# Issuing the table loads of the state space model's pairs from GpSimd in place of SyncE

## The chip, the core and the metric

The program runs on one core of one Trainium2 chip. The metric is the device time of one execution, in microseconds (us), over the median of several executions. The core has the engines TensorE (PE in the profile, with its weight loads as PEld), VectorE (DVE), ScalarE (ACT), GpSimd (POOL) and SyncE (SP). Each of them takes its instructions strictly in the order in which they were put into its queue; an instruction that waits holds up all that stands behind it on the same engine. In this kernel SyncE computes nothing: it issues DMA transfers.

## The reference

Two layers of a hybrid backbone over 640 tokens (128 context, 512 latent). In each layer one input projection feeds three head groups that run beside each other: a state space model (SSM), neighbourhood attention and grouped query attention. One output projection and a gated feed-forward network follow. The SSM is a diagonal complex recurrence in 16 groups of 16 channels with 64 states, run forward and backward:

```
def ssm_mixer(u, lp, h0_f, h0_b):
    ...
    for d, (h0, rev) in ...:
        lam_bar, b_bar = ssm_discretize(lp['ssm_lam_re'][d], lp['ssm_lam_im'][d], ...)
        hs = ssm_scan(uf, lam_bar, b_bar, h0, rev)
        y = y + jnp.einsum('blgp,gcp->blgc', hs, c_mat).real
        finals.append(hs[:, 0] if rev else hs[:, -1])
    g = jax.nn.gelu(y.reshape(b, n, SSM_WIDTH))
    out = g * jax.nn.sigmoid(g @ lp['w_ssm_glu'])
```

## The kernel before

The kernel is one program for both layers. Weights come from HBM through SyncE (`wload`, L293 to L302, and others), are split by ScalarE and by VectorE or GpSimd into a rounded high part and a low remainder (`split`, L280 to L284: the high part on L283, the remainder on L284), and are multiplied on TensorE in three passes (`mm3`, L309 to L313). On GpSimd, L284 is the remainder for a part of the weights; in groups called `wl` it feeds the third pass.

The SSM (`ssm`, L669) works in chunks: 640 tokens are 80 columns of 8 tokens, and the 16 groups are taken as 8 pairs. `ssm_tables` (L429) computes the tables of each pair ahead and stores them in DRAM: V (input to state, 128x512), R (rotation, 128x320), C (state to output, 128x512) and Z (the part within a chunk, two times 128x8x16). For each pair:

- `front` (L692 to L718) takes three buffers a, b, c of one pool of ten (`k4`). It loads V and C into b (L697, L699) and R and Z into a (L698, L709 twice). Z is read in pieces of 64 bytes, 128x8 of them in each of its two loads. GpSimd copies the decay factors into a third part of a (L703) and clears four columns of them (L705, two instructions). PE multiplies the inputs with V (L714); ScalarE copies the result into c (L716).
- `turn` transposes it on PE (L724). `rotate` works on DVE: L732 and L738 rotate, the scan on L742 is the recurrence (it reads the copied and cleared factors of a), L747, L748 and L753 rotate back.
- `back` multiplies on PE with C (L767, 8 matmuls, which the profile counts as 16) and Z (L770, 2, counted as 4); ScalarE copies the result out (L772).

`front` of the next pair is put after `turn` of the current one. Ten buffers are few: b of a pair comes free when L767 of the pair two before is done, and a when L770 of it is done (for pair 6, a was held by a bias table that DVE's L948 reads).

The order of the instructions on every engine is set by the Tile framework: the program is written in stages that yield to each other (`layer`, L1358, runs the grouped query attention with the SSM's pairs, weight pieces of the input projection and the modulation weights between its steps, and then the neighbourhood attention with the last pairs), and a scheduler with a timeline of its own sets the final order from it (`schedule_with_timeline_sim=True`, L1911). So a change of one engine moves instructions on the others too.

Beside the SSM the profile's rows name: L381, modulation weights `wa` on PE; L859, transposes; L942 to L953, L978 and L853, neighbourhood attention; L1266, a store of ScalarE's tile `zt`.

Of the kernel before, what the change touches and what calls it, by code (L numbers as in the profile page):

```python
# [157 lines left out]
class Build:  # L158
# [510 lines left out]
    def ssm(self, l, zu, T, out):  # L669

        nc, I = self.nc, self.I
        V, S, G = nc.vector, nc.scalar, nc.gpsimd
# [3 lines left out]
        for m in range(2):  # L676
            ug = self.k4()[:, 0:SLAB].rearrange("p (g j) -> p g j", g=8)
            src = zu[m * 128:(m + 1) * 128].rearrange("(g c) (t j) -> t c g j", c=16, t=8)
# [13 lines left out]
        def front(pair):  # L692
            a, b, c = self.k4(), self.k4(), self.k4()
            rot, rml, tm = a[:, 0:320], a[:, 320:640], a[:, 640:896]
            tv, tcb = b[:, 0:512], b[:, 512:1024]
            vs = c[0:NJ, 0:512]
            nc.sync.dma_start(tv, T["V"][pair])  # L697
            nc.sync.dma_start(rot, T["R"][pair].rearrange("p w d e -> p (w d e)"))  # L698
            nc.sync.dma_start(tcb, T["C"][pair])  # L699
            r8 = T["r8"][:, 2 * pair:2 * pair + 2].unsqueeze(2).unsqueeze(3).broadcast_to([128, 2, 2, NJ])  # L700

            rv = rml.rearrange("p (d w j) -> p d w j", d=2, w=2)
            G.tensor_copy(rv, r8)  # L703
            for d, e in ((0, 16), (1, 64)):
                G.memset(rv[:, d, :, 0:e + 1:e], 0.0)  # L705
            for gg in range(2):
                zz = T["Z"][2 * pair + gg]
                src = bass.AP(tensor=zz.tensor, offset=zz.offset, ap=[[16, 128], [256, 8], [1, 16]])
                nc.sync.dma_start(tm[:, gg * 128:(gg + 1) * 128].rearrange("p (t c) -> p t c", t=8), src)  # L709
            g0 = (pair % 4) * 2  # L710
            ug = ugs[pair // 4][:, g0:g0 + 2, :]
            sp = self.psM()
            for gg in range(2):
                nc.tensor.matmul(sp[0:NJ, gg * 256:(gg + 1) * 256], lhsT=ug[:, gg, :],  # L714
                                 rhs=tv[:, gg * 256:(gg + 1) * 256], start=True, stop=True)
            S.copy(vs.rearrange("p (q g n) -> p g q n", q=4, g=2), sp[0:NJ].rearrange("p (g q n) -> p g q n", g=2, q=4))  # L716
            return rot.rearrange("p (w d e) -> p w d e", w=2, d=2), rml, tcb, tm, ug, vs, c
# [42 lines left out]
        def back(pair, sx, rot, rml, tcb, tm, ug, vs, c):  # L760
# [10 lines left out]
            for hf in range(2):  # L771
                S.copy(ysb[hf][0:NJ, :, pair * 32:(pair + 1) * 32].rearrange("p t (g c) -> p g t c", g=2),  # L772
                       yp.rearrange("p g (t c) -> p g t c", t=8)[:, :, hf * 4:hf * 4 + 4, :])

        nxt = front(0)
        yield
        sx = None
        for pair in range(NPAIR):
            cur = nxt
            vt = turn(*cur)  # L780
            if pair + 1 < NPAIR:
                nxt = front(pair + 1)
            sx = rotate(pair, vt, *cur)
            yield
            back(pair, sx, *cur)
            if pair + 1 < NPAIR:
                yield
# [16 lines left out]
        for hf in range(2):  # L804
            for ch in range(2):
# [4 lines left out]
                src = pt[:, 0:4 * NJ].rearrange("p (t j) -> p t j", t=4)  # L810
# [1104 lines left out]
```

## Time and profile before

| | us |
|---|---|
| median of 3 executions | 1797.16 (1796.97 to 1809.3) |
| profiled execution, its own time | 1788.01 |
| its span | 1786.0 |
| PE busy | 1641.2 (92%) |
| DVE busy | 1222.5 (68%) |
| ACT busy | 827.3 (46%) |
| POOL busy | 763.5 (43%) |
| mean granted clock of TensorE | 0.96 |

The profiled execution is 9 us below the median of the others. Matmuls overlap by their pipeline, so a busy share of 92% on PE does not say that 8% could be had. The SSM's pairs run in two stretches: their loads are issued from 163.8 to 320.8 us in layer 0, and in layer 1 from 1042.3 us (pair 0 alone), and then from 1088.2 to 1202.4 us. The rest of the time holds projections and the feed-forward network.

### The profile page before, as it was taken

The numbers are of one execution on the slowest core, as the hardware profiler recorded it, in microseconds if no ns is written. First come the engines' busy times: TensorE is split into PE (matmuls) and PEld (weight loads), VectorE is DVE, ScalarE is ACT, GpSimd is POOL, SyncE is SP. The second block draws the span as 40 slices with busy tenths as digits, with TensorE's granted clock in tenths as the row PEclk, the third lists the DMA queues.
The fourth block names the chain that finished last, engine by engine and source line by source line (L and its number), as shares of the span: only waits on it lengthen the run. The fifth ranks groups of instructions, "written<-read, shape, count | busy, mean of one in ns | idle before, by whom it ended". The sixth has DMA issues, their size and how long they took to land. (4 is left out here: it accounts for less than half of the span.)

```text
span 1786.0 us, 31489 instructions
## 1 busy us (share of the span) xinstructions
PE 1641.2 (92%) x11624; PEld 1435.8 (80%) x11624; DVE 1222.5 (68%) x2460; ACT 827.3 (46%) x1800; POOL 763.5 (43%) x651
## 2 busy tenths in 40 slices
PE   5899899898899999999897989998979999999997
PEld 2898677676788888798796978876859899998995
DVE  5765546627678776778877565565487687876777
ACT  5444446657443334243345556665574242433433
POOL 3853203059235343346266232111785254454463
PEclk9999899798999999999999999998989999999999
DMA  9445767446353645232324243463542231222212
GB/s 335 112 126 139 238 194 213 123 158 203 107 172 122 195 127 182 81 121 71 121 85 157 92 129 96 111 187 115 180 148 85 94 107 59 92 74 69 98 62 81
DMA packets 183114, 234.90 MB, mean 132 GB/s; under 512 B 78960, under 2 KB 112048, under 8 KB 182960
## 3 DMA queue, kind: packets, MB, share of 16 engines
q1 hardware_dynamic: 182960, 232.88, 42.3%
q8 instruction: 92, 1.51, 0.3%
q14 instruction: 62, 0.51, 0.1%
HBM read 203.57 MB, written 29.39 MB: 130 GB/s over the span
## 5 line engine op out<-in xcount | busy, mean ns | idle before, releaser
L284 POOL TENSOR_TENSOR wl<-wr,wh 128x512 fp32r<-128x512 f32 x362 | 504.2, 1413 | 522.8 <-ACT wh L283 343.2
L283 ACT CAST wh<-wr 128x512 fp32r<-128x512 f32 x450 | 275.2, 619 | 383.9 <-DVE wr L1597 88.6
L311 PE MATMUL psM<-hh,wh 128*128 128x320 f32 x560 | 180.3, 322 | 2.3 <-DVE ys L1647 1.1
L313 PE MATMUL psM<-hh,wl 128*128 128x320 f32 x560 | 177.9, 318 | 0.0
L312 PE MATMUL psM<-hl,wh 128*128 128x320 f32 x560 | 177.8, 318 | 0.0
L311 PEld LDWEIGHTS psM<-hh,wh 128*128 128x128 f32 x560 | 108.5, 194 | 6.2 <-issue 1.8
L311 PE MATMUL psT<-hh,wh 128*128 128x320 f32 x352 | 109.9, 312 | 0.0
L313 PEld LDWEIGHTS psM<-hh,wl 128*128 128x128 f32 x560 | 108.6, 194 | 1.5 <-issue 1.4
L312 PE MATMUL psT<-hl,wh 128*128 128x320 f32 x352 | 109.2, 310 | 0.0
L313 PE MATMUL psT<-hh,wl 128*128 128x320 f32 x352 | 109.0, 310 | 0.0
L312 PEld LDWEIGHTS psM<-hl,wh 128*128 128x128 f32 x560 | 108.7, 194 | 0.3
L230 POOL TENSOR_TENSOR sm<-sm,mhalf 128x1 f32<-128x1 f32 (+2 forms) x46 | 54.3, 1182 | 92.3 <-DVE sm L260 49.3
L1647 DVE TENSOR_TENSOR ys<-ys,psM 128x320 f32<-128x320 f32 x140 | 65.0, 481 | 33.8 <-PE psM L313 31.9
L1160 DVE TENSOR_REDUCE psS<-psS 128x1 f32<-128x640 f32 x64 | 52.7, 828 | 47.4 <-PE psS L1157 45.6
L1647 DVE TENSOR_TENSOR ys<-ys,psT 128x320 f32<-128x320 f32 x140 | 65.0, 481 | 28.8 <-PE psT L313 27.7
L311 PE MATMUL psT<-b,wh 128*128 128x320 f32 x240 | 76.5, 319 | 8.3 <-DVE ys L1647 7.4
L311 PE MATMUL psM<-b,wh 128*128 128x320 f32 x240 | 76.1, 317 | 5.8 <-DVE ys L1647 5.8
L284 POOL TENSOR_TENSOR wl<-ws,wh 128x512 fp32r<-128x512 f32 x40 | 53.6, 1340 | 64.4 <-ACT wh L283 62.6
L859 PE MATMUL psT<-ident,ys 128*128 128x128 f32 x440 | 73.2, 285 | 5.8 <-DVE hl L284 3.3
L311 PE MATMUL psM<-wh,xs 128*128 128x512 f32 x190 | 74.9, 394 | 3.7 <-DVE k L1771 3.5
L311 PE MATMUL psT<-wh,xs 128*128 128x512 f32 x190 | 75.6, 398 | 2.9 <-DVE k L1771 2.9
L1597 DVE TENSOR_TENSOR ws<-wr,wr 128x512 f32<-128x512 f32 x40 | 37.0, 926 | 58.9 <-DMA wr<-in_w_ffn_in_dram 28.3
(440 smaller groups left out, 4907.9 us busy)
## 6 DMA issues: line engine op xcount, KB each, us to landing
wr<-in_w_ffn_in_dram SPq DMA_DIRECT2D x88, 512.0 KB, 3.7
ev<-in_w_ada_dram SPq DMA_DIRECT2D x112, 256.0 KB, 4.0
wr<-in_w_ffn_out_dram SPq DMA_DIRECT2D x40, 512.0 KB, 3.9
wr<-in_w_out_dram SPq DMA_DIRECT2D x32, 512.0 KB, 3.6
wr<-in_w_in_dram SPq DMA_DIRECT2D x28, 512.0 KB, 4.8
wa<-in_w_ada_dram SPq DMA_DIRECT2D x24, 512.0 KB, 4.7
k<-in_x_dram SPq DMA_DIRECT2D x10, 512.0 KB, 5.6
xs<-zqk SPq DMA_DIRECT2D x32, 160.0 KB, 3.7
```

The source lines that it names most:

```text
L230: self.nc.gpsimd.tensor_tensor(out=o, in0=v, in1=self.mhalf.broadcast_to([128, v.shape[1]]), op=ALU.pow)
L283: nc.scalar.copy(hi, src)
L284: (lo_eng or nc.vector).tensor_tensor(out=lo, in0=src, in1=hi.bitcast(F32), op=ALU.subtract)
L311: nc.tensor.matmul(ps, lhsT=ah, rhs=bh, start=first, stop=False)
L312: nc.tensor.matmul(ps, lhsT=ah, rhs=bl, start=False, stop=False)
L313: nc.tensor.matmul(ps, lhsT=al, rhs=bh, start=False, stop=last)
L859: self.nc.tensor.transpose(pt[:, j * 128:(j + 1) * 128], s, self.ident)
L1160: V.tensor_reduce(out=m, in_=sp[:, :, 0:320], axis=AX.XY, op=ALU.max, negate=True)
L1597: V.tensor_tensor(out=o, in0=x, in1=y, op=op)
L1647: V.tensor_tensor(out=o, in0=x, in1=y, op=ALU.add)
```

## The change

The five loads of `front` are issued by GpSimd (`G` is `nc.gpsimd`) in place of SyncE. Eight pairs in two layers make 80 transfers.

```
-            nc.sync.dma_start(tv, T["V"][pair])
-            nc.sync.dma_start(rot, T["R"][pair].rearrange("p w d e -> p (w d e)"))
-            nc.sync.dma_start(tcb, T["C"][pair])
+            G.dma_start(tv, T["V"][pair])
+            G.dma_start(rot, T["R"][pair].rearrange("p w d e -> p (w d e)"))
+            G.dma_start(tcb, T["C"][pair])
...
-                nc.sync.dma_start(tm[:, gg * 128:(gg + 1) * 128].rearrange("p (t c) -> p t c", t=8), src)
+                G.dma_start(tm[:, gg * 128:(gg + 1) * 128].rearrange("p (t c) -> p t c", t=8), src)
```

Three places show how the order moved. The first is GpSimd's queue at the last two pairs of layer 0. `k_697` and `k_696` are the buffers b and a of pair 6, `k_711` and `k_710` those of pair 7; `xs_4044` belongs to the attention.

```order
+L697 DMA k_697_3842<-tabV_306 128x512
+L699 DMA k_697_3842<-tabC_307 128x512
 L891 MEMSET xs_4044 128x64
+L698 DMA k_696_3841<-tabR_309 128x320
 L703 COPY k_696_3841<-r_65_310 128x320
+L709 DMA k_696_3841<-tabZ_308 128x8x16 x2
+L697 DMA k_711_3936<-tabV_306 128x512
+L699 DMA k_711_3936<-tabC_307 128x512
+L698 DMA k_710_3935<-tabR_309 128x320
+L703 COPY k_710_3935<-r_65_310 128x320
+L709 DMA k_710_3935<-tabZ_308 128x8x16 x2
 L705 MEMSET k_696_3841 128x2x2 x2
```

Before, the two memsets of pair 6 (last row) followed the copy of pair 6 at once; now Z of pair 6 and all that pair 7 loads stand between them. Layer 1 has the same order at its last two pairs.

The second place is PE's queue between the first matmul of pair 7 and L767 of pair 6 in layer 0. `k_711` and `k_697` are again b of pairs 7 and 6, `k_698` the buffer c with the result of pair 6's scan; the other rows are the attention's.

```order
+L859 MATMUL psT_4071<-ident,ys_3873 128x128 x4
+L714 MATMUL psM_3946<-k_711_3936,k_433_2377 80x256 x2
+L859 MATMUL psT_4077<-ident,ys_3873 128x128 x2
+L859 MATMUL psT_4158<-ident,ys_3967 128x128 x4
+L724 MATMUL psM_4107<-ident,k_712_3937 128x80 x4
+L978 MATMUL psT_4077<-ys_4070,xs_3757 64x128 x4
+L978 MATMUL psT_4077<-ys_4070,k_672_3751 64x128 x2
+L853 MATMUL psT_4077<-ident,sm_3889 64x128 x2
 L767 MATMUL psS_4094<-k_697_3842,k_698_3843 80x128
```

L714 and L724 of pair 7 stood ahead of L767 of pair 6 before too, some rows earlier; the rows of L859, L978 and L853 stood behind it. In layer 1 six such rows of L859 moved ahead of L767 of pair 6.

The third place is GpSimd's queue at pair 4 of layer 0, with `k_621` and `k_620` as its b and a. The rows of L284 are remainders of weights.

```order
 L284 TENSOR_TENSOR wl_3234<-wr_3231,wh_3233 128x512
+L697 DMA k_621_3438<-tabV_306 128x512
+L698 DMA k_620_3437<-tabR_309 128x320
+L699 DMA k_621_3438<-tabC_307 128x512
+L703 COPY k_620_3437<-r_65_310 128x320
+L709 DMA k_620_3437<-tabZ_308 128x8x16 x2
 L284 TENSOR_TENSOR wl_3238<-wr_3231,wh_3237 128x512
 L284 TENSOR_TENSOR wl_4451<-wr_4448,wh_4450 128x512
-L703 COPY k_620_3437<-r_65_310 128x320
```

The pair's loads now stand ahead of the remainder `wl_3238`, which before followed `wl_3234` directly. On PE its first use stands 64 rows behind the last row of L767 of pair 2; before, it stood 13 rows behind.

## Rows read from the trace of the kernel before

**Rows 1.** The page: span, and busy time of each engine.

```profile
span 1786.0 us, 31489 instructions
PE 1641.2 (92%) x11624; PEld 1435.8 (80%) x11624; DVE 1222.5 (68%) x2460; ACT 827.3 (46%) x1800; POOL 763.5 (43%) x651
```

**Rows 2.** Windows: start:end, length, busy PE, PEld, DVE, ACT, POOL, clock, DMA.

```profile
163.00:345.00 182.00, 162.13 (x1544) 131.41 (x1542) 107.31 (x267) 94.07 (x247) 34.15 (x52) 0.93 0.71 203
1088.00:1204.00 116.00, 112.29 (x962) 97.55 (x961) 72.66 (x188) 72.18 (x191) 22.90 (x39) 0.97 0.53 144
```

**Rows 3.** Waits of PE, 163 to 345 us: total, times, longest.

```profile
PE psM L381 <- DMA wa<-in_w_ada_dram: 6.4, 5, 2.5
```

**Rows 4.** Waits of SP's queue, the same stretch.

```profile
SPq L697 <- PE psS L767: 7.4, 3, 4.4
```

**Rows 5.** Lines L697 and L709: issue, ns minimum/median/maximum, first to last start.

```profile
L697 SPq DMA_DIRECT2D k<-tabV x16: 319/370/1170, 163.8 to 1199.8; - x16
L709 SPq DMA_DIRECT2D k<-tabZ x32: 425/532/1034, 171.0 to 1202.4; - x32
```

**Rows 6.** DMA issues: KB each, median us from issue to landing.

```profile
k<-tabV SPq DMA_DIRECT2D x16, 256.0 KB, 3.3
k<-tabZ SPq DMA_DIRECT2D x32, 64.0 KB, 4.0
```

**Rows 7.** Groups of POOL by shape: busy us, mean ns, idle before.

```profile
L284 POOL TENSOR_TENSOR wl<-wr,wh 128x512 fp32r<-128x512 f32 x362 | 504.2, 1413 | 522.8 <-ACT wh L283 343.2 <-DVE wl L284 113.7 <-DMA ev<-in_w_ada_dram 33.0
...
L703 POOL COPY k<-r 128x320 f32<-128x320 f32 x16 | 8.7, 545 | 59.1 <-PE psS L770 30.1 <-DMA tabC<-k 15.5 <-DVE ys L948 8.8
...
L705 POOL MEMSET k<- 128x4 f32 x32 | 2.3, 105 | 0.8
```

**Rows 8.** Timeline of layer 0's last pairs: start, length, engine; SP and POOL.

```profile
316.63 0.32 SPq L698 DMA_DIRECT2D k<-tabR  x1
316.67 0.45 POOL L703 COPY k<-r 128x320 f32<-128x320 f32 x1 [1.02 <-DVE ys L948]
```

**Rows 9.** The same stretch: DVE, from the scan of pair 6.

```profile
326.56 0.82 DVE L742 TENSOR_TENSOR_SCAN k<-k,xs 128x320 f32<-128x320 f32 x1
...
327.54 0.48 DVE L747 TENSOR_TENSOR xs<-k,k 128x320 f32<-128x320 f32 x1
...
329.20 0.69 DVE L753 TENSOR_TENSOR k<-xs 128x80 f32<-128x80 f32 x4
```

**Rows 10.** The same stretch: PE, from L767 of pair 6.

```profile
331.01 0.71 PE L767 MATMUL psS<-k,k 64*80 64x128 f32 x2
...
338.81 0.66 PE L859 MATMUL psT<-ident,ys 128*128 128x128 f32 x4
...
340.36 0.66 PE L978 MATMUL psT<-ys,xs 128*64 128x128 f32 x8
...
341.39 0.50 PE L942 MATMUL psS<-b,b 128*128 128x256 f32 x2
```

**Rows 11.** Layer 1: copy of pair 6 on POOL, L767 of pair 6 on PE.

```profile
1196.34 0.45 POOL L703 COPY k<-r 128x320 f32<-128x320 f32 x1 [7.76 <-DVE ys L948]
...
1212.70 0.71 PE L767 MATMUL psS<-k,k 64*80 64x128 f32 x2
```

**Rows 12.** Pair 4 of layer 0: L767 of pair 2, and PE's spacing.

```profile
274.17 0.44 PE L767 MATMUL psS<-k,k 64*80 64x128 f32 x2
...
277.64 0.31 PE L311 MATMUL psM<-hh,wh 128*128 128x320 f32 x1
277.79 0.31 PE L312 MATMUL psM<-hl,wh 128*128 128x320 f32 x1
```

**Rows 13.** POOL's timeline: remainders before pair 4, copy of pair 5.

```profile
267.48 4.99 POOL L284 TENSOR_TENSOR wl<-wr,wh 128x512 fp32r<-128x512 f32 x4 [21.27 <-ACT wh L283]
...
292.57 1.19 POOL L703 COPY k<-r 128x320 f32<-128x320 f32 x1 [3.28 <-ACT b L1179]
```

## The prediction

> **What bounds the kernel now.** I read the page's first lines, then the windows of the two stretches in which the pairs run, then the waits of PE and of SP's queue there, and last the timeline of the places where the change puts something in another engine's way. TensorE is busy for 1641.2 of 1786.0 us [rows 1], and in the two stretches for 162.13 of 182 and 112.29 of 116 us [rows 2]. So PE is the bound, and what it idles there (19.9 and 3.7 us) is all that could be won in these stretches. The largest wait of PE for a DMA is the one for modulation weights, 6.4 us in five waits [rows 3]; SyncE issues them. SyncE's own queue stands for 7.4 us in front of V loads whose buffer PE has not yet freed [rows 4]. POOL is busy for 34.15 us of 182 and 22.90 of 116 [rows 2], so it has room as a whole; what stands behind a load in its queue decides.
>
> **What goes and what comes.** SyncE loses 80 issues. By the medians one issue of V takes 0.37 us and one of Z 0.53 us [rows 5]; with R and C priced as V, a pair takes 3 x 0.37 + 2 x 0.53 = 2.2 us of SyncE. That time is on no path of its own. Its value is that SyncE no longer stands before a full buffer, so weights behind it start earlier. Bounds: nothing, and all 6.4 us of [rows 3]. I take 2 us, about a third: the pairs' loads are only one of several things that hold that queue.
>
> POOL gains the 80 issues, and no row shows what one costs there. From below it is SyncE's own, 2.2 us a pair. From above, POOL would be held until the load has landed: 3.3 us for each of V, R, C and 4.0 us for each Z [rows 6], 17.9 us a pair. My value goes by POOL's own rows: a fixed part of 0.5 us, near the copy's 0.545 and above the memset's 0.105, and a part that grows with the pieces, 1413 ns over 512 steps, that is 2.76 ns each [rows 7]. Taking one step for one piece is the estimate in it. V, R and C have 128 pieces (0.85 us each), Z has 1024 (3.3 us each), so a pair takes 3 x 0.85 + 2 x 3.3 = 9.15 us. Sixteen pairs are 146 us; with eight of them the first stretch holds 73 + 34 of 182 us, so POOL's sum is not the bound.
>
> The steps of POOL's rows show a price for each further piece, 2.76 ns in [rows 7]. The Trainium skill (DMA: Bandwidth & Descriptors, section "Anatomy of one DMA — SWDGE (gpsimd) path") speaks for the opposite on this path: one can emit a lot of descriptors before the incremental cost shows up. By that rule a Z load would cost what a V load does, and the sum below would be -2 us instead of +4.7; no row of this kernel shows a load issued by POOL, so the rule is one of the rivals.
>
> **The last two pairs of a layer.** The order puts the memsets of pair 6 behind the loads of pair 7, and the scan of pair 6 reads what they clear. In layer 0 the load of R for pair 6 waits, as now, until 316.63 us, when its buffer is free [rows 8]. From there POOL has R 0.85, the copy 0.45 [rows 8], two Z 6.6, V, C and R of pair 7 2.55, a copy 0.45, two Z 6.6, together 17.5 us: the memsets come at 334.1 us. The scan began at 326.56 us [rows 9]. From its start to the end of L753 the parts are 0.82, 0.48 twice (L748 is like L747) and 0.69 us [rows 9], 2.5 us, so PE's L767 of pair 6 can begin at 336.6 us; it began at 331.01 us [rows 10], 5.6 us earlier. The new order fills part of it: ten rows of L859 at 0.66 us for four, 1.65 us, and the rows of L978 and L853 from 340.36 to 341.39 us, 1.03 us [rows 10], now stand ahead of it. 5.6 - 2.7 = 2.9 us is left. That V of pair 7 comes later as well (issued by 325.3 us) lies inside this wait.
>
> In layer 1 the same copy began at 1196.34 us; 17.5 us of POOL and 2.5 us of DVE lead to 1216.3 us, against 1212.70 us for L767 [rows 11]: 3.6 us, less six rows of L859 (1.0 us), 2.6 us. The two ends together cost 5.5 us.
>
> **Pair 4 of layer 0.** One remainder of weights now stands behind the pair's five loads, whose first waits until L767 of pair 2 is done at 274.6 us [rows 12]. 9.15 us of loads, 0.45 of copy and 1.25 of the remainder (4.99 us for four [rows 13]) give 285.5 us. PE has 64 rows to do before it needs the remainder; at the spacing of 0.15 us [rows 12] that is 9.6 us, until 284.2 us. The wait is 1.3 us; I take 1.2. At the other pairs POOL's work waits too, but I found either idle time on POOL behind it or PE rows put ahead, and set it at nothing; if that cover is gone, each costs at most what a pair's loads take beyond it.
>
> **The sum** is 5.5 + 1.2 - 2 = +4.7 us on the profiled execution, from 1788.0 to 1792.7 us. That execution lies 9 us under the median of the runs, 1797.16, so I forecast 1797.2 + 4.7 = 1802 us.
>
> **The rivals.** *POOL is held longer (slower).* If each load holds POOL until it has landed, the 17.5 us on POOL become 4 x 3.3 + 4 x 4.0 + 0.9 = 30.1 us, 12.6 us more at each end of a layer, and pair 4 waits 8.75 us longer: 4.7 + 25.2 + 8.75 = 38.7 us, 1836 us. For it speaks that POOL does its instructions one at a time; against it, that SyncE's issue takes 0.37 us where the landing takes 3.3 [rows 5, 6]. It decides (18 us, 1%) where a pair costs 12.6 us in place of 9.15, reckoned evenly between the two sums.
>
> *An issue is as cheap as on SyncE (not slower).* Then the row at the end of a layer is 4 x 0.37 + 4 x 0.53 + 0.9 = 4.5 us, the memsets come at 321.1 us, 5 us ahead of the scan, pair 4 has 4 us of loads and remainder against 9.6, and only the relief is left: 1795 us with 2 us, 1791 us if all waits for modulation weights go. With the many pieces of Z at the price of V the row is 8 x 0.85 + 0.9 = 7.7 us, the memsets come at 324.3 us, still ahead of the scan, and the time is the same 1795 us. More than 1% faster would need 18 of the 23.6 us of idle time; I see no mechanism for that.
>
> *VectorE's work stretches POOL's issues (slower).* POOL's copies show that it happens to POOL: 1.19 us in one place against a mean of 0.545 [rows 7, 13], 0.65 us more. If every load suffers this, the eight at each end of a layer cost 5.2 us more and the five at pair 4 3.2 us: 4.7 + 13.6 = 18.3 us, 1815 us. DVE is busy for 107 of 182 us [rows 2], which speaks for some of them, not for all. The Trainium skill (SBUF — State Buffer, the box on the "DVE blocks DMA" trap, and its example of 620 ns alone and 3100 ns beside a VectorE copy) has the reason for such a stretch: GpSimd writes the descriptors of its own transfers and cannot while VectorE holds the shared port. By its example each of the 21 loads would be 2.48 us longer and the time about 1854 us; no row here shows a load on POOL, and the copies show less.
>
> **How the numbers follow.** About 1% (18 us) is what a measurement of this kernel can tell from no change. Chances: forecast, with a pair between 6 and 12.6 us, 0.45 (1795 to 1815 us); cheap issue in either form 0.25 (1791 to 1795); held longer than 12.6 us a pair 0.18 (1815 to 1836, and above if more remainders come late); stretched by VectorE 0.12 (1805 to 1830). Slower by over 1% comes from the held case, 0.18, and most of the last, 0.09: 0.27. Faster by over 1% is left with 0.05, from a better order by chance; within 1% the rest, 0.68. The range leaves out the fastest tenth, below 1788, and what lies above the held case's middle, 1834.
>
> **What would show it.** In the changed profile: a second queue with 80 transfers; the length of L697 against L709 on POOL (0.85 and 3.3 us by my estimate; equal lengths speak for the cheap case, 3.3 and 4.0 for the held one). POOL's memset of pair 6 about 17.5 us after R of pair 6 in both layers, DVE idle before the scan until then, and PE idle before L767 of pair 6 for 3 us. At pair 4 a wait of PE on L284 of about 1 us. PE's waits for modulation weights below 6.4 us. I am wrong if the memset comes before DVE reaches the scan, or if PE waits elsewhere for remainders or for attention inputs that POOL makes between the pairs.

## The result, and the profile after

The changed kernel takes 1821.06 us (median of 3, 1820.36 to 1823.28) against 1797.16 us: ratio 1.0135, 95% interval 1.0096 to 1.0173. That is slower by about 1.35%; the interval begins just below 1%. It lies inside the range (1788 to 1834), 19 us above the forecast of 1802.

The page after, lines that answer to [rows 1], and GpSimd's new queue:

```profile
span 1819.2 us, 31508 instructions
PE 1658.0 (91%) x11624; PEld 1446.4 (80%) x11624; DVE 1228.5 (68%) x2460; ACT 821.7 (45%) x1796; POOL 816.2 (45%) x731
...
q1 hardware_dynamic: 142768, 219.77, 38.4%
q0 software_dynamic: 4352, 13.11, 2.7%
```

The span is 33.2 us longer. About 9 us of that is chance: the trace of before is of an execution 9 us below its median, the trace of after of one at its median. The same 11624 matmuls keep PE busy for 16.8 us longer, and it idles for 16.4 us more (161.2 against 144.8). Most of both happens in the stages in which the pairs run. I cut each trace by the count of PE's matmuls: "layer 0" runs from the start of the 1200th to that of the 3000th, "layer 1" from the 7250th to the 8750th. These are the two windows, of before and of after (columns as in [rows 2]):

```profile
165.30:399.60 234.30, 212.00 (x1803) 170.06 (x1801) 124.52 (x307) 123.43 (x313) 58.54 (x70) 0.93 0.65 190
1068.30:1268.70 200.40, 191.61 (x1506) 161.47 (x1501) 115.53 (x300) 122.93 (x318) 43.94 (x55) 0.94 0.46 133
```

```profile
168.70:415.50 246.80, 221.36 (x1802) 176.61 (x1801) 126.00 (x307) 122.05 (x312) 82.56 (x109) 0.89 0.58 180
1084.40:1299.70 215.30, 199.37 (x1504) 167.86 (x1502) 119.64 (x299) 120.61 (x318) 68.29 (x91) 0.90 0.42 124
```

They are 12.5 and 14.9 us longer, 27.4 of the 33.2 us. PE's busy time takes 17.1 us of it, at a granted clock of 0.89 and 0.90 in place of 0.93 and 0.94; idle time takes 10.3 us. So in these two traces over half of it is not waiting: it is matmuls that ran at 1.2 in place of 2.4 GHz.

**What a load costs GpSimd.** The issue lines of after (ns minimum/median/maximum), for [rows 5]:

```profile
L697 POOL DMA_DIRECT2D k<-tabV x16: 561/579/764, 167.1 to 1224.3; - x16
```

```profile
L698 POOL DMA_DIRECT2D k<-tabR x16: 537/543/552, 173.5 to 1225.4; - x16
```

```profile
L699 POOL DMA_DIRECT2D k<-tabC x16: 536/541/552, 174.1 to 1224.8; - x16
```

```profile
L709 POOL DMA_DIRECT2D k<-tabZ x32: 887/895/912, 175.4 to 1227.2; - x32
```

A pair takes 0.579 + 0.543 + 0.541 + 2 x 0.895 = 3.45 us, and 16 pairs 55 us; POOL's busy time grew by 52.7 us. The loads land about as before (KB each, median us from issue to landing), for [rows 6]; R takes 3.3 us (before 3.1) and C 4.2 (before 3.9):

```profile
k<-tabV POOLq DMA_DIRECT2D x16, 256.0 KB, 3.2
...
k<-tabZ POOLq DMA_DIRECT2D x32, 64.0 KB, 3.6
```

**Pair 4 of layer 0.** POOL's timeline of after, for [rows 13] (start, length):

```profile
276.98 1.28 POOL L284 TENSOR_TENSOR wl<-wr,wh 128x512 fp32r<-128x512 f32 x1 [2.00 <-ACT wh L283]
278.20 0.58 POOL L697 DMA_DIRECT2D k<-tabV  x1
...
280.24 1.78 POOL L709 DMA_DIRECT2D k<-tabZ  x2
282.04 5.00 POOL L284 TENSOR_TENSOR wl<-wr,wh 128x512 fp32r<-128x512 f32 x4
```

The remainder `wl_3238` is the first of the four in the last line: done at about 283.3 us. In before it ended with the batch of [rows 13], at 272.5 us. PE does not stand still for it. But the rows of PE's order around the transposes of pair 3 show what was moved (equal matmuls that follow each other are one row). Before:

```
L313 MATMUL psM_3241<-hh_367,wl_3238 128x320
...
L313 MATMUL psM_3350<-hh_367,wl_3238 128x320
L724 MATMUL psM_3432<-ident,k_575_3191 128x80 x4       (row 1173)
```

After, with 13 other rows between the first passes of the two pieces and the last:

```
L312 MATMUL psM_3350<-hl_368,wh_3237 128x320           (row 1165)
...
L313 MATMUL psM_3241<-hh_367,wl_3238 128x320           (row 1179)
...
L313 MATMUL psM_3350<-hh_367,wl_3238 128x320           (row 1186)
...
L724 MATMUL psM_3432<-ident,k_575_3191 128x80 x4       (row 1192)
```

`psM` has two buffers (`psM()`, bufs=2). The pieces `psM_3241` and `psM_3350` of the input projection hold both until their last pass with `wl_3238` is done, and L724 of pair 3 needs one. PE's timeline: in before it started at

```profile
280.28 0.44 PE L724 MATMUL psM<-ident,k 80*128 80x80 f32 x4
```

and in after at 289.61 us, behind the last passes:

```profile
286.48 0.39 PE L313 MATMUL psM<-hh,wl 128*128 128x320 f32 x1
...
289.61 0.50 PE L724 MATMUL psM<-ident,k 80*128 80x80 f32 x4
```

From here the pairs are late: L767 of pair 3 starts at 298.5 us (before 287.6), L767 of pair 7 ends at 354.2 us (before 339.8). Of each of these differences 3.4 us were there when the stretch began (168.7 us against 165.3), so L724 of pair 3 is about 6 us late within it. Its later place cost PE nothing there, since PE did other work; that work is then missing under later waits.

Part of it can be named: 24 matmuls of the attention, as the profile counts them (20 of L1184, 4 of L853). In before they stand behind L724 of pair 4, and so run while that pair's chain is on VectorE:

```profile
296.59 0.44 PE L724 MATMUL psM<-ident,k 80*128 80x80 f32 x4
296.96 1.31 PE L1184 MATMUL psT<-b,b 128*64 128x128 f32 x20
298.11 0.39 PE L853 MATMUL psT<-ident,sm 128*64 128x128 f32 x4
```

In after they are done over 6 us ahead of it:

```profile
297.06 1.31 PE L1184 MATMUL psT<-b,b 128*64 128x128 f32 x20
298.20 0.39 PE L853 MATMUL psT<-ident,sm 128*64 128x128 f32 x4
...
305.12 0.44 PE L724 MATMUL psM<-ident,k 80*128 80x80 f32 x4
```

L767 of pair 4 stands at the same place among PE's matmuls in both (the 2464th), so 1.5 us of work are gone from under this chain, and its L767 waits. The waits of PE, 163 to 352 us (total, times, longest), for [rows 3] on the second line:

```profile
PE psS L767 <- DVE k L753: 5.5, 3, 4.6
PE psM L381 <- DMA wa<-in_w_ada_dram: 3.5, 4, 1.9
```

One of them shows how idle time and clock hang together. Timelines of VectorE, GpSimd and PE at pair 4, and the windows around the wait:

```profile
306.51 4.01 DVE L738 TENSOR_TENSOR xs<-xs 128x158 f32<-128x158 f32 x2
```

```profile
305.31 5.03 POOL L284 TENSOR_TENSOR wl<-wr,wh 128x512 fp32r<-128x512 f32 x4
```

```profile
313.18 0.71 PE L767 MATMUL psS<-k,k 64*80 64x128 f32 x2 [4.64 <-DVE k L753]
```

```profile
296.00:308.50 12.50, 12.37 (x111) 10.49 (x109) 8.52 (x15) 6.82 (x19) 7.01 (x9) 1.00 0.37 113
308.50:313.20 4.70, 0.06 (x2) 0.02 (x1) 4.54 (x11) 0.17 (x1) 1.92 (x4) 0.89 0.93 260
313.20:320.00 6.80, 6.80 (x32) 5.35 (x32) 4.42 (x15) 2.90 (x9) 1.13 (x2) 0.50 0.30 88
320.00:330.00 10.00, 9.54 (x32) 6.62 (x32) 6.96 (x15) 4.12 (x10) 0.15 (x1) 0.50 0.95 277
```

L738 usually takes 0.55 us; beside GpSimd's batch it takes 4.01 and ends as the batch does. PE idles for 4.6 us, and then works for 16.8 us at a granted clock of 0.50, that is 1.2 GHz: L714 of pair 6 takes 1.91 us for four rows there, where it took 1.09 us at full clock. Such a spell is no mark of the loss, though: in two of the kernels below that do not lose layer 0 the clock is 0.50 at the same place for 20 us (303.0 to 323.4 us with only Z on GpSimd, 306.9 to 327.4 with the fills ahead of the loads).

**The last pairs.** POOL after, for [rows 8], and the scan of pair 6 on DVE, for [rows 9]:

```profile
330.98 0.54 POOL L698 DMA_DIRECT2D k<-tabR  x1 [3.93 <-DVE sm L956]
...
338.34 0.22 POOL L705 MEMSET k<- 128x4 f32 x4
```

```profile
345.84 0.81 DVE L742 TENSOR_TENSOR_SCAN k<-k,xs 128x320 f32<-128x320 f32 x1
```

From R to the memsets it is 7.4 us, and the scan comes 7.3 us after them. In layer 1 (for [rows 11]) R is issued at 1221.06 us, the memset at 1228.08 and the scan at 1235.17.

### The profile page after: what moved, and what is told of

It reads as the page before. It is cut to its first block, busy times and chain, and to the rows that moved or that the text cites. A ratio compares the mean times of both kernels' runs of the same rounds, so it can differ in the third digit from the quotient of the medians.

```text
span 1819.2 us, 31508 instructions
## 1 busy us (share of the span) xinstructions
PE 1658.0 (91%) x11624; PEld 1446.4 (80%) x11624; DVE 1228.5 (68%) x2460; ACT 821.7 (45%) x1796; POOL 816.2 (45%) x731
## 3 DMA queue, kind: packets, MB, share of 16 engines
q1 hardware_dynamic: 142768, 219.77, 38.4%
q0 software_dynamic: 4352, 13.11, 2.7%
## 5 line engine op out<-in xcount | busy, mean ns | idle before, releaser
L284 POOL TENSOR_TENSOR wl<-wr,wh 128x512 fp32r<-128x512 f32 x362 | 503.1, 1411 | 497.0 <-ACT wh L283 343.0
L230 POOL TENSOR_TENSOR sm<-sm,mhalf 128x1 f32<-128x1 f32 (+2 forms) x46 | 55.0, 1197 | 97.2 <-DVE sm L260 49.1
L1647 DVE TENSOR_TENSOR ys<-ys,psM 128x320 f32<-128x320 f32 x140 | 64.9, 481 | 34.2 <-PE psM L313 32.3
L1647 DVE TENSOR_TENSOR ys<-ys,psT 128x320 f32<-128x320 f32 x140 | 65.0, 481 | 29.8 <-PE psT L313 28.7
L284 POOL TENSOR_TENSOR wl<-ws,wh 128x512 fp32r<-128x512 f32 x40 | 53.6, 1341 | 65.7 <-ACT wh L283 65.7
L1160 DVE TENSOR_REDUCE psS<-psS 128x1 f32<-128x640 f32 x64 | 52.7, 829 | 42.0 <-PE psS L1157 40.8
L859 PE MATMUL psT<-ident,ys 128*128 128x128 f32 x440 | 74.4, 291 | 5.0 <-DVE sm L1192 1.7
```

Source lines behind the costliest of these rows:

```text
L230: self.nc.gpsimd.tensor_tensor(out=o, in0=v, in1=self.mhalf.broadcast_to([128, v.shape[1]]), op=ALU.pow)
L284: (lo_eng or nc.vector).tensor_tensor(out=lo, in0=src, in1=hi.bitcast(F32), op=ALU.subtract)
L859: self.nc.tensor.transpose(pt[:, j * 128:(j + 1) * 128], s, self.ident)
L1160: V.tensor_reduce(out=m, in_=sp[:, :, 0:320], axis=AX.XY, op=ALU.max, negate=True)
L1647: V.tensor_tensor(out=o, in0=x, in1=y, op=ALU.add)
```

## The experiments

Three theories stood at the start: GpSimd's time per issue is what costs; the new order, in which the loads stand ahead of other work on GpSimd, is what costs; or any edit here makes the scheduler throw a new order, and times scatter by chance. The letters in the expectations were given anew from group to group, so the conclusions use words. The table holds all runs; "pair 3" is the time from the start of L714 of pair 2 to that of L724 of pair 3, and the last two columns are the stretches defined above, worked out from each trace by counting PE's matmuls. Each ratio is to executions of before taken in the same group: the median of before was 1797.16 us for after, 1799.74 for the next four, 1798.73 from "layer 0 alone" to "R, Z", and 1800.25 for the rest. The stretches are of one execution each.

| kernel | ratio to before (95%) | pair 3, us | layer 0, us | layer 1, us |
|---|---|---|---|---|
| before | 1 | 47.5 | 234.3 | 200.4 |
| after | 1.0135 (1.0096 to 1.0173) | 56.0 | 246.8 | 215.3 |
| only Z on GpSimd | 1.0005 (0.9984 to 1.0026) | 48.7 | 230.7 | 200.2 |
| only V, R, C | 0.9978 (0.9958 to 0.9998) | 48.8 | 227.8 | 203.4 |
| all on ScalarE | 1.0033 (1.0005 to 1.0062) | 51.4 | 235.9 | 199.7 |
| before, lines of R and C exchanged | 0.9982 (0.9962 to 1.0002) | 47.7 | 233.4 | 197.6 |
| layer 0 alone | 1.0081 (1.0055 to 1.0107) | 54.7 | 246.9 | 202.1 |
| layer 1 alone | 1.0066 (1.0039 to 1.0093) | 49.9 | 241.2 | 206.7 |
| R, C, Z | 1.016 (1.014 to 1.018) | 53.9 | 249.1 | 206.7 |
| R, Z | 1.0019 (0.9994 to 1.0044) | 49.1 | 238.1 | 202.6 |
| fills ahead of the loads | 1.0044 (1.0014 to 1.0074) | 49.3 | 236.6 | 208.1 |
| pair 4 on SyncE | 1.0162 (1.0114 to 1.021) | 51.1 | 244.0 | 215.4 |
| after, w_out remainders on VectorE | 1.0133 (1.0086 to 1.018) | 56.1 | 250.4 | 207.2 |
| before, the same edit | 0.9992 (0.9961 to 1.0022) | 47.5 | 235.0 | 202.1 |

**Only Z, and only V, R, C.** The first puts L697 to L699 back on `nc.sync`, the second L709.

```
-            G.dma_start(tv, T["V"][pair])          (and R, C)
+            nc.sync.dma_start(tv, T["V"][pair])    (and R, C)
```

> Only the two Z loads of each pair are issued by GpSimd, V, R and C stay on SyncE. Theory A (head of the line: remainders of weights on GpSimd stand behind loads that wait for a buffer, run late and in one batch, and hold up VectorE and then PE): the Z loads wait for buffer a, so remainders can still be held back; between +8 and +25 us against before (1805 to 1822). Theory B (the order that the scheduler plans anew makes the difference, whoever issues): any value from -10 to +25 us, unrelated to which loads moved. Theory C (the price of the issues themselves, 2 x 0.895 of 3.4 us per pair): half of the 24 us, 1809.

> Only V, R and C of each pair are issued by GpSimd, the Z loads stay on SyncE. Theory A (head of the line): V waits for buffer b at the head of GpSimd's queue as in the full change, so nearly the full loss, 1812 to 1822 us. Theory B (a newly planned order): any value from -10 to +25 us against before. Theory C (price of the issues, 1.7 of 3.4 us per pair): half of the 24 us, 1809.

1800.16 and 1795.0 us. L709 of the first kernel:

```profile
L709 POOL DMA_DIRECT2D k<-tabZ x32: 880/886/1078, 174.8 to 1212.8; - x32
```

So the 1.77 us of a pair's Z loads are on GpSimd at the same price, and cost nothing; nor do the other three loads (1.66 us). The price of an issue doesn't add up to the loss: the two halves give 0, the whole 24 us.

**All five on ScalarE, and an order changed for no reason.** In the first `S.dma_start` stands on the five lines. The second is the kernel before with one exchange:

```
             nc.sync.dma_start(tv, T["V"][pair])
-            nc.sync.dma_start(rot, ...)
             nc.sync.dma_start(tcb, T["C"][pair])
+            nc.sync.dma_start(rot, ...)
```

> All five loads of each pair are issued by ScalarE in place of SyncE. GpSimd's queue holds no load. Theory A (head of the line on GpSimd): the batch of remainders is not held back, so GpSimd's part is gone; ScalarE's own work can stand behind the waiting loads instead, which is worse, since ScalarE makes the high parts of all weights and feeds PE: 1797 to 1830 us, with PE waiting for ScalarE and no VectorE instruction stretched to 4 us. Theory B (a newly planned order): any value from -10 to +25 us. Theory C (price of GpSimd's issues): no loss, 1797 us.

> The kernel before with the lines of R and C exchanged in the program, all on SyncE: the work is the same, the scheduler plans a new order. Theory A (head of the line on GpSimd) and theory C (price of GpSimd's issues): the same as before within 5 us, 1792 to 1802. Theory B (a newly planned order makes the difference): it can be off by 10 us and more.

1805.41 and 1793.57 us. The issues of the first:

```profile
L697 ACTq DMA_DIRECT2D k<-tabV x16: 338/338/587, 165.8 to 1212.4; - x16
```

```profile
L709 ACTq DMA_DIRECT2D k<-tabZ x32: 377/494/1622, 173.1 to 1214.5; - x32
```

Taking the loads off SyncE is neither a gain nor a loss of size. In these two kernels the re-drawn order moved the time by some 0.2 to 0.3%, far from 1.35%; two draws do not exclude a rarer, larger one.

**One layer alone.**

```
-            G.dma_start(tv, T["V"][pair])                               (all five)
+            (G if l == 0 else nc.sync).dma_start(tv, T["V"][pair])      (l == 1 in the other)
```

> The full change in layer 0 alone; in layer 1 SyncE issues the loads as before. Its order in layer 0 is that of the full change, and in layer 1 that of the kernel before. Theory A2 (in layer 0 a remainder of the input projection stands behind pair 4's loads on GpSimd; its late passes hold both PSUM banks of the tag that the transposes of pair 3, L724, need, so L724 of pair 3 starts some 9 us later than before and every later pair with it): layer 0 ends 10 to 15 us late, so 1808 to 1815 us. Theory B (a newly planned order scatters by itself): between 1793 and 1806, the scatter of the runs so far. Theory D (the loss is one of layer 1 only): no change, 1797 to 1803.

> The full change in layer 1 alone; layer 0 has the order of the kernel before, layer 1 that of the full change. If the losses of the two layers add up, this and the run with layer 0 alone share the 21 to 24 us between them: 1808 to 1813 us here, with the loss between the first matmul of pair 0 and the transposes that follow the SSM. Theory B: between 1793 and 1806. If layer 1 only inherits what layer 0 did (clock or order), no loss here.

1809.53 and 1808.86 us. Each layer brings its part, 0.8% and 0.7%, about the whole together. Windows of the two stretches, the kernel with layer 0 alone:

```profile
166.90:413.80 246.90, 218.72 (x1803) 173.84 (x1802) 126.07 (x307) 122.63 (x312) 82.78 (x109) 0.90 0.59 179
1086.60:1288.70 202.10, 192.93 (x1506) 162.10 (x1502) 114.50 (x299) 120.98 (x316) 43.97 (x55) 0.94 0.47 131
```

Layer 0 has all of after's length, layer 1 is that of before. In the other kernel layer 0 has 241.2 us, more than any other kernel with SyncE's order in that layer: the stretch scatters from 227.8 to 241.2 us where its pair 3 is in time.

**R, C and Z; R and Z.** V on SyncE in the first, V and C in the second.

```
-            G.dma_start(tv, T["V"][pair])
+            nc.sync.dma_start(tv, T["V"][pair])
-            G.dma_start(tcb, T["C"][pair])          (second kernel only)
+            nc.sync.dma_start(tcb, T["C"][pair])
```

> R, C and Z of each pair on GpSimd, V on SyncE. In its order the transposes of pair 3 in layer 0 stand as late as in the full change (behind the held banks, row 1191 of PE's order, 1192 in the full change, 1173 before). Theory A2: L724 of pair 3 at 288 to 291 us in place of 280, layer 0 ends late by 8 to 15 us, 1806 to 1821 in all. Theory E (the wait for V at the head of GpSimd's queue is the cause): V is off GpSimd, but C waits for the same buffer, so the same. Theory C (price of the issues, 2.9 of 3.4 us per pair): 1817. Theory B: 1793 to 1806.

> R and Z of each pair on GpSimd, V and C on SyncE: one load fewer on GpSimd than in the run with R, C and Z. In its order the transposes of pair 3 in layer 0 stand as before (row 1174, before 1173). Theory A2: L724 of pair 3 at 279 to 284 us, no loss in layer 0, 1793 to 1803 in all. Theory C (price of the issues, 2.3 of 3.4 us per pair): 1813. Theory B: 1793 to 1806, so only the place of L724 tells it from A2 here.

1824.55 and 1800.2 us. C alone, 0.54 us of GpSimd a pair, makes the step from nothing to the whole loss. In PE's order L724 of pair 3 stands at row 1191 in the first and 1174 in the second (1192 after, 1173 before). So the loss does not grow with the sum of the prices, but jumps with the order. A threshold of the sum, between 2.33 and 2.87 us of GpSimd a pair, would fit these rows too; the next kernel tells the two apart.

**The same five loads, remainder ahead of them.** If the jump is the cause, it must be possible to keep all 80 issues on GpSimd and not lose layer 0. The three loads are written behind the copy and the memsets, and the scheduler then puts `wl_3238` ahead of pair 4's loads:

```
-            G.dma_start(tv, T["V"][pair])           (and R, C)
             ...
             G.tensor_copy(rv, r8)
             ... G.memset(rv[:, d, :, 0:e + 1:e], 0.0)
+            G.dma_start(tv, T["V"][pair])           (and R, C)
```

> The changed kernel with one edit in front(pair): the three loads L697 to L699 are written behind the copy L703 and the memsets L705, ahead of the two Z loads. All five loads of all 16 pairs are still issued by GpSimd (80 issues, 3.45 us a pair by the rows of the changed kernel). What moves is their place: in layer 0 the w_in remainder wl_3238 now stands ahead of pair 4's loads in GpSimd's order, and L724 of pair 3 stands at row 1175 of TensorE's order (1173 before the change, 1192 with it). Theory A, the loads that push the remainder back hold TensorE's two psM buffers and make L724(3) late: layer 0 is healed, L724(3) comes 48 to 50 us behind L714(2) in place of 56.0, and the time is that of the run with layer 1 alone changed or less, 1797 to 1810, ratio 1.000 to 1.007. Theory B, the issues themselves, 3.45 us a pair on GpSimd, cost the time: nothing of them is taken away, 1818 to 1824, ratio 1.012 to 1.016. Theory C, the schedule scatters by chance: anything from 1793 to 1824, with no tie to L724(3).

1807.48 us. POOL at pair 4 (loads are L703 to L705 here, the copy L700), PE's L724 of pair 3, and the windows:

```profile
275.21 2.53 POOL L284 TENSOR_TENSOR wl<-wr,wh 128x512 fp32r<-128x512 f32 x2 [1.63 <-ACT wh L283]
277.68 0.45 POOL L700 COPY k<-r 128x320 f32<-128x320 f32 x1
278.07 0.55 POOL L703 DMA_DIRECT2D k<-tabV  x1
```

```profile
279.74 0.23 PE L724 MATMUL psM<-ident,k 80*128 80x80 f32 x1
```

```profile
169.80:406.40 236.60, 214.84 (x1803) 171.62 (x1802) 126.52 (x307) 120.98 (x312) 83.63 (x108) 0.93 0.62 187
1080.60:1288.80 208.20, 186.36 (x1506) 158.51 (x1504) 123.46 (x299) 120.62 (x318) 67.98 (x90) 0.94 0.44 128
```

Layer 0 is back at 236.6 us and a clock of 0.93 with POOL as busy as in after (83.63 against 82.56 us). The issues are the same, only their place moved, at all 16 pairs: 10 of the 12.5 us are gone. The ratio 1.0044 lies in the 1.000 to 1.007 that the order's theory gave, outside the 1.012 to 1.016 of the prices'. Layer 1 keeps 7.7 us.

**Pair 4 alone on SyncE.**

```
-            G.dma_start(tv, T["V"][pair])                                  (all five)
+            (nc.sync if pair == 4 else G).dma_start(tv, T["V"][pair])
```

> The changed kernel, but the five loads of pair 4 of either layer are issued by SyncE; those of the other seven pairs stay on GpSimd. L724 of pair 3 stands at row 1184 of TensorE's order, half way between 1173 (before) and 1192 (changed). Theory A, L724(3) held back behind the w_in pieces: about half of layer 0's loss comes back, L724(3) at 51 to 53 us behind L714(2), 1808 to 1815, ratio 1.006 to 1.010; layer 1 keeps its loss. Theory B, GpSimd's issues: one pair in eight is taken off, an eighth of the loss, 1817 to 1820. Theory C, chance: no tie to the row.

1825.36 us: the theory of the order expected 1808 to 1815, and missed. Its place did what was expected (pair 3 at 51.1 us, of 51 to 53), and the stretch took 244.0 us, less than after, but only 2.8 of 12.5 us came back; layer 1 stayed at 215.4. In its profile the stretches outside the two take 5.3 us more than in after. Outside the two stretches the kernels of the table scatter by that much in any case (the stage between them from 666.9 to 679.9 us, without a pattern in the loads). So the start of L724 of pair 3 is not proportional to the loss. Nor do the two `psM` buffers explain this kernel: in PE's order its last passes with `wl_3238` are back at rows 1158 to 1173, ahead of L724 of pair 3 at 1184, so the remainder holds nothing up, and most of layer 0's loss stays. What it shares with after are the 24 matmuls: L1184 runs at 298.79 us, ahead of L724 of pair 4 at 301.82.

**VectorE's stall as a suspect.** The wait of 4.64 us with the stalled L738 could be the cause rather than the late pair. `LO` decides who computes the remainders of the w_out weights, the batches of up to 5 us on GpSimd; both kernels get the edit:

```
-    LO = (True, True)
+    LO = (False, False)
```

> The changed kernel with LO at L1522 set to (False, False): the remainders of the w_out weights (L284 in batches of up to 5 us on GpSimd, 4 in a row) are computed by VectorE in place of GpSimd, in both layers. L724(3) stays at row 1192. Theory A1, the loss is the late L724(3) alone: the time stays where the changed kernel is in comparison with its own partner, the kernel before with the same edit (the next run), 1.0 to 1.6% above that one. Theory A2, a good part of the loss is VectorE's stalls beside GpSimd's batches late in the stage (L738 4.01 us in place of 0.55, TensorE waiting 4.64 us at L767): the difference to the partner falls to 0.5% or less. VectorE takes some 1.2 to 2.5 us for each of these remainders in place of GpSimd, so both may be slower than their originals by some per mille.

> The kernel before with LO at L1522 set to (False, False): partner of the run ahead of it, with the five loads on SyncE and L724(3) at row 1173. Theory A1 expects it 1.0 to 1.6% below that run, theory A2 0.5% or less below it. Against the kernel before itself: VectorE takes over the remainders of w_out, which no stage of the trace shows it short of time for, so between 0.995 and 1.008.

1820.6 and 1796.47 us, 1.3% apart (1820.6 / 1796.47 = 1.0134). L738 of pair 4 in the changed kernel with the edit, and windows of layer 0 with it, for the changed kernel and then for the kernel before:

```profile
309.18 0.55 DVE L738 TENSOR_TENSOR xs<-xs 128x158 f32<-128x158 f32 x2
```

```profile
169.10:419.50 250.40, 223.99 (x1803) 178.44 (x1802) 134.56 (x328) 121.87 (x312) 58.23 (x89) 0.88 0.58 177
```

```profile
167.60:402.60 235.00, 212.59 (x1802) 171.28 (x1801) 133.40 (x328) 121.21 (x312) 32.86 (x50) 0.92 0.65 189
```

The stall is gone, the loss is not. The opposite case is the kernel with the fills ahead: there one L738 took 5.05 us, and layer 0 was healed. The stall is one of the places where the late chain shows, and not the cause of the loss.

**What is shown and what is open.** In layer 0 the four kernels whose pair 3 takes over 53 us have 246.8 to 250.4 us; the eight below 50 us have 227.8 to 241.2; of the two between, one has 235.9 and one 244.0. The place of the 24 matmuls sorts all fourteen: in after, layer 0 alone, R, C and Z, pair 4 on SyncE, and after with the remainders on VectorE they stand ahead of L724 of pair 4, and the stretch takes 244.0 to 250.4 us; in the nine others they stand behind it, and it takes 227.8 to 241.2. PE waits 2.6 to 4.7 us at L767 of pair 4 in the five, at most 1.8 in the nine. PE's idle time in the stretch parts the same way (23.9 to 28.5 us against 16.0 to 22.4), its busy time does not (218.7 to 224.0 against 210.4 to 220.3); so the longer busy time at a lower clock, over half of the difference between the traces of before and after, also comes without the loss.

That in layer 0 the place of the loads in GpSimd's queue decides, and not their price, is shown by the kernel with the fills ahead (ratio 1.0044 against 1.0135, the intervals apart). It moves the loads of all pairs; that pair 4's place alone does it is not shown, and the kernel with pair 4 on SyncE speaks against it. That the two `psM` buffers tie the pieces to L724 in after is read from the order, not tried with a third buffer. The 24 matmuls were not put back by themselves either, so their part is a match over fourteen traces and not a test.

In layer 1 the six kernels that load at least R, C and Z there from GpSimd have 206.7 to 215.4 us, the eight others 197.6 to 203.4, so the loss is real; what begins it I could not settle. After's waits there are many small ones (L978 for `ys` 3.6 us, L714 for V 2.5, L1157 for `ys` 2.4, L714 for L1271 2.0), and the others show different ones. The traces say where it falls: after is 6.1 us behind before at the 1000th matmul of the stretch and 15.0 at the 1300th, that is over the last three pairs. The order differs there too: in all six L724 of pair 5 stands 58 matmuls further ahead than in all eight.

## Why the prediction was right or wrong

**The bound and the room** held: POOL's added 53 us as a sum bound nothing, and the loads landed about as before.

**The price of an issue** was too high: 9.15 us a pair, measured 3.45, between SyncE's 2.2 and my value. The fixed part (0.5 us) was right; the part per piece was not: 0.541 us with 128 pieces and 0.895 with 1024 make 0.4 ns for each further piece, not the 2.76 ns that I took from the steps of L284. The rule I set against it (the Trainium skill, DMA: Bandwidth & Descriptors, section "Anatomy of one DMA — SWDGE (gpsimd) path": many descriptors before the incremental cost shows up) points the right way, since 896 pieces more cost 0.35 us; but that cost does show, a Z load holding GpSimd for 1.65 times as long as a C load, and the time by the rule, 1795 us, was not measured.

**The last two pairs** (+5.5 us): the order was read rightly, but the row on POOL took 7.4 and 7.0 us, not 17.5. The memsets come 7 us ahead of the scan in both layers, so the wait that I priced did not come. I had named just this as a sign that I am wrong.

**Pair 4** (+1.2 us): the place was right, and this is the step that failed. I priced the moved remainder as a wait of PE: ready time against the 64 rows of cover. Its ready time (283.3 us, forecast 285.5) was even earlier, and no such wait came. What I left out is that the scheduler had paid in the order already: the covering rows were rows moved ahead. L724 of pair 3 stood 19 rows further back, and 24 matmuls that had covered the chain of pair 4 (VectorE's rotation and scan, from L724 to PE's L767) were done before it began. PE then waited 4.6 us at that L767, and layer 0's stretch took 12.5 us more. One kernel that only moves GpSimd's loads takes back about 10 of these, so the place of the loads is the cause there; that it acts through the buffers held by the remainder is not shown.

**The other pairs** (set at nothing): layer 1 lost 14.9 us where I had 2.6. It is not the same slip, since L724 of pair 5 moved ahead there; which step failed in it stays open.

**SyncE's relief** (-2 us): PE's wait for modulation weights fell from 6.4 us [rows 3] to 3.5, 2.9 us less. Right in sign and size as far as one trace each tells, and lost in the rest.

**The clock** was in no term. Of the 27.4 us in the two stretches 17.1 are longer busy time at a lower granted clock. I priced waits at their length; here idle time was followed by matmuls at half the clock.

**The rivals.** POOL held until landing fell at 0.54 us against 3.2. VectorE stretching POOL's loads fell too: V's longest issue is 0.764 us against a median of 0.579 (the first V, beside two operations of L617), Z's 0.912 against 0.895. The Trainium skill (SBUF — State Buffer, section "A bandwidth-pool intuition that's wrong (but worth ruling out)") gives 620 and 3100 ns for a load beside a VectorE copy; no load here shows it, but in after's trace the only VectorE copy within SBUF beside a load was one of L740, for 0.06 us, so that case was hardly met. The cheap issue was the right one in its mechanism, 26 us off in its time. "Within 1%" had 0.68 of my chances and "slower" 0.27; the slower end, 1834, came from rivals whose mechanisms did not occur. That 1821 us lies inside the range is therefore luck. The prices differed between my cases, the order of PE was in none of them.

## What to carry to other kernels

When an edit moves an instruction to another engine under a scheduler, compare the whole order of the bound engine, not only the rows next to the move: look for the head of a serial chain that slipped back, for buffers held by work that now waits for its last input, and for filler that moved from behind the chain's head to ahead of it. Price a chain by the filler that is left under its waits. Take more than one trace of a kernel before reading a cause from its clock. Before choosing the queue for a load, ask what stands behind it there; a cheap issue (0.5 to 0.9 us) can still cost some 10 us by its place.

## What the runs showed of the hardware

- A load issued by GpSimd holds it for 0.54 us with 128 pieces and 0.895 us with 1024. One of the 80 was lengthened beside VectorE's work, by 0.19 us (the first V). SyncE's own medians are 0.37 and 0.53 [rows 5], ScalarE's 0.34 and 0.49.
- By the profile's count the 80 loads are 4352 packets on GpSimd's queue (q0 above). On SyncE's queue they were 40192, the difference of q1 between before and after (142768, above):

```profile
q1 hardware_dynamic: 182960, 232.88, 42.3%
```

- VectorE's operations with two inputs in SBUF can be held up beside GpSimd's L284 batches: L738 took 4.01 us in place of 0.55 and ended within 0.2 us of the batch (310.52 and 310.34 us). I had looked for the contention in the other direction. An operation with one input in PSUM did not: of two of one shape in after, L1663 (both inputs in SBUF) took up to 1641 ns and L1647 never over 490, though about half of its 280 ran beside L284 (ns minimum/median/maximum):

```profile
L1663 DVE TENSOR_TENSOR ys<-ys,ys x40: 473/1282/1641, 527.0 to 1786.1; 128x320 f32<-128x320 f32 x40
L1647 DVE TENSOR_TENSOR ys<-ys,psM x140: 469/481/490, 512.1 to 1784.5; 128x320 f32<-128x320 f32 x140
```

- After 4.6 idle us TensorE's granted clock was 0.50 for 16.8 us of nearly unbroken work, and L714 took 1.91 in place of 1.09 us. The length of the wait does not give that of the spell: with only Z on GpSimd waits of 1.6 and 1.0 us stand at the start of 20.4 us at 0.50.
